# Running sums on POOL, q's squares in two fp32r parts, and low parts of 24 weight tiles by accumulating DMA, in a four-layer trunk

## The chip, the cores and the metric

One Trainium2 chip, one core in use. The metric is device time of the kernel, in microseconds, least is best. What is compared is the median of several runs of each kernel.

## The reference

Four residual layers over a sequence of 512 tokens of width 1024, in fp32. Layers 0 and 3 are Conformer convolution modules, layer 1 is attention with a forget gate, layer 2 a short gated convolution. Each is wrapped in an RMS norm and widens to 2048.

```python
def conformer_conv_mixer(h, w_in, conv_w, conv_b, ln_g, ln_b, w_out):
    proj = h @ w_in
    val, glu_gate, z = jnp.split(proj, 3, axis=-1)
    u = val * jax.nn.sigmoid(glu_gate)
    u = causal_depthwise_conv(u, conv_w) + conv_b
    u = jax.nn.silu(layer_norm(u, ln_g, ln_b))
    return (u * jax.nn.silu(z)) @ w_out
...
def forgetting_attention_mixer(h, w_in, f_bias, q_norm_g, k_norm_g, w_out):
    ...
    q = rms_norm(q.reshape(b, s_len, FOX_HEADS, FOX_HEAD_DIM), q_norm_g)
    k = rms_norm(k.reshape(b, s_len, FOX_HEADS, FOX_HEAD_DIM), k_norm_g)
    ...
for i in range(DEPTH):
    x = x + Mixer(rms_norm(x, norm))
```

The conformer's convolution has 31 taps and 2048 channels, attention has 16 heads of 128.

## The kernel before

**Tiles.** Everything is held with channels on the 128 partitions and the 512 tokens along the free axis. x is 8 tiles of 128x512, a branch 16. The weights are cut into 289 chunks of 128x1024 (512 KB): per conformer 48 for the input projection (16 each of val, gate and z) and 16 for the output, 65 + 16 for attention, 64 + 16 for the short convolution. Chunks 0 to 63 are layer 0, 225 to 288 layer 3.

**Two-part products.** A product of near fp32 accuracy is made of three fp32r products. Each chunk is loaded into w_raw (3 buffers, by SyncE's queue), ScalarE casts it to w_hi, and POOL subtracts to get w_lo = w_raw - w_hi (outside the conformers POOL or VectorE; 4 buffers each of hi and lo). The activations are split in the same way (hh and hl, or hn_hi and hn_lo after a normalisation, g_hi and g_lo ahead of the output). `project` then issues 24 matmuls for a chunk: 8 of hi by hh, 8 of hi by hl, 8 of lo by hh. With `fine` each of the 24 is planned alone, for the first tile of a layer, whose inputs come one after the other. `chunk` splits chunks AHEAD = 3 tiles before the tile that is projected.

**The plan.** Nothing runs in the order of the source. Each operation is entered with its estimated cost on the engines that can run it, a priority (its number, less a boost), its reads and writes; `Plan.trace` then simulates the engines with these costs and gives every engine its list, which it works through in order. A change of an operation, a cost or a priority can so move operations everywhere.

**Norms.** The mean of squares over channels is a sum over partitions: a matmul with a constant matrix (ones_d, ones_e in fp32, ones_hr in fp32r). `Stream.add` makes one square per x tile; in layer 0 each square goes to TensorE as a fp32 matmul of its own (ms, 8 of them), in the other layers the middle ones are first added up, leaving two.

**Conformer.** Order of tiles (`a_order`): val and gate of tile i, and from tile 9 on z of tile i - 9, so that the last nine tiles of the input projection are z alone. The first four tiles use the raw x and are multiplied by rstd afterwards, the others the normalised hn. The convolution of a tile is made of taps on VectorE (cv, into PSUM) and 7 taps on ScalarE and POOL (prod, pacc); tiles 7, 12 and 15 go to TensorE with matrices pw, through two trips to memory (ua to ud to phases, then oa to od to ob). The result of tile i is d_i. `count_in` adds d_i into s1 and its square into s2 on POOL; the last two (DIRECT = 2, tiles 14 and 15) go to TensorE directly: the layer norm's sums are meanp <- s1, d14, d15 and e2p <- s2, sq14, sq15, three fp32 matmuls each. The norm that comes out of it is applied to d, multiplied with sz = silu(z), and the output projection o starts.

**Queries.** `queries` projects a head's q, squares it and sums the squares over the 128 channels with four fp32 matmuls whose weights are the squares and whose moving operand is one column of ones (qs).

## Time and profile before

| | us |
|---|---|
| median of 3 runs | 1793.65 (1792.62 to 1793.85) |
| the profiled execution | 1794.22 |
| its span | 1792.3 |
| TensorE busy in it | 1767.3 (99%) |
| VectorE, ScalarE, POOL busy | 1167.2, 866.7, 1096.9 |
| TensorE clock granted (mean) | 0.999 |

The layers follow each other: layer 0 up to about 404 us, attention to 964, the short convolution to 1402, the second conformer to the end. Times in rows are microseconds from the start of the span. A row of the timeline gives start, length, engine, line of the code, operation, what is written and read by the program's names, shapes, a count where several are taken together, and in brackets the idle time before it and what ended that. The chain of waits is the chain of work that ended last, followed back from the last instruction. A matmul on fp32 operands is two instructions in the profile, one on fp32r operands is one.

### The profile page before, as it was taken

The numbers are of one execution on the slowest core, as the hardware profiler recorded it, in microseconds if no ns is written. First come the engines' busy times: TensorE is split into PE (matmuls) and PEld (weight loads), VectorE is DVE, ScalarE is ACT, GpSimd is POOL, SyncE is SP. The second block draws the span as 40 slices with busy tenths as digits, with TensorE's granted clock in tenths as the row PEclk, the third lists the DMA queues.
The fourth block names the chain that finished last, engine by engine and source line by source line (L and its number), as shares of the span: only waits on it lengthen the run. The fifth ranks groups of instructions, "written<-read, shape, count | busy, mean of one in ns | idle before, by whom it ended". The sixth has DMA issues, their size and how long they took to land.

```text
span 1792.3 us, 21883 instructions
## 1 busy us (share of the span) xinstructions
PE 1767.3 (99%) x8196; PEld 1462.4 (82%) x8196; DVE 1167.2 (65%) x1690; ACT 866.7 (48%) x1255; POOL 1096.9 (61%) x654
## 2 busy tenths in 40 slices
PE   8999999999999999999999999999999999999999
PEld 6788887888888888888788888888888878878787
DVE  6999997736777777867523333333313699999770
ACT  6656655536555555656433222222223564755550
POOL 5999998865333333544454555455445599989882
PEclk9999999999999999999999999999999999999999
DMA  6243432233222222222222222222223224334222
GB/s 219 83 154 99 141 135 83 94 106 118 83 78 91 85 77 85 75 77 71 71 95 94 94 94 100 101 94 95 96 100 123 88 94 147 106 129 136 94 94 71
DMA packets 63065, 182.40 MB, mean 102 GB/s; under 512 B 7136, under 2 KB 13280, under 8 KB 62960
## 3 DMA queue, kind: packets, MB, share of 16 engines
q1 hardware_dynamic: 62960, 181.02, 29.9%
q8 instruction: 64, 1.05, 0.2%
q14 instruction: 41, 0.34, 0.1%
HBM read 175.71 MB, written 5.28 MB: 101 GB/s over the span
## 4 chain that ended last, share of the span: by engine, by line
PE 81%; DVE 16%; POOL 1%; issue 1%; DMA 1%; ACT 0%; SPq 0%; DVEq 0%; POOLq 0%; ACTq 0%
PE o L379 19%; PE z L379 17%; DVE cv L341 13%; PE k L379 5%; PE v L379 5%; PE u L379 5%; PE c L379 5%; PE b L379 5%; PE q L379 5%; PE gate L379 3%; PE val L379 3%; PE cv L379 2%; PE op L379 2%; PE lg L379 2%; PE pt L874 1%
## 5 line engine op out<-in xcount | busy, mean ns | idle before, releaser
L413 POOL TENSOR_TENSOR w_lo<-w_raw,w_hi 128x1024 fp32r<-128x1024 f32 x274 | 661.1, 2414 | 586.2 <-PE z L379 110.0
L315 ACT CAST w_hi<-w_raw 128x1024 fp32r<-128x1024 f32 x289 | 303.2, 1050 | 550.9 <-issue 137.1
L341 DVE SCALAR_TENSOR_TENSOR cv<-u,vt,cv 128x495 f32<-128x495 f32 (+24 forms) x608 | 447.2, 736 | 19.7
L330 POOL TENSOR_TENSOR pacc<-prod,pacc 128x510 f32<-128x510 f32 (+5 forms) x148 | 174.7, 1181 | 11.1 <-ACT prod L317 4.4
L330 DVE TENSOR_TENSOR x<-o,x 128x512 f32<-128x512 f32 x32 | 21.2, 687 | 200.9 <-PE o L379 200.9
L317 ACT ACTIVATE prod<-u,vt 128x510 f32<-128x510 f32 (+8 forms) x166 | 106.9, 709 | 46.3 <-DVE u L330 46.3
L379 PE MATMUL o<-g_hi,w_hi 128*128 128x512 f32 x512 | 127.9, 391 | 0.7 <-DVE z L330 0.7
L379 PE MATMUL o<-g_lo,w_hi 128*128 128x512 f32 x512 | 127.0, 389 | 0.0
L379 PE MATMUL o<-g_hi,w_lo 128*128 128x512 f32 x512 | 126.7, 389 | 0.0
L379 PEld LDWEIGHTS o<-g_hi,w_hi 128*128 128x128 f32 x512 | 95.8, 188 | 21.7 <-DVE z L330 1.5
L379 PEld LDWEIGHTS o<-g_hi,w_lo 128*128 128x128 f32 x512 | 96.0, 188 | 19.9
L379 PEld LDWEIGHTS o<-g_lo,w_hi 128*128 128x128 f32 x512 | 95.9, 188 | 19.8
L246 ACT ACT_TABLE_LOAD x70 | 89.8, 1283 | 1.9 <-PEq L1030 0.7
L330 DVE TENSOR_TENSOR z<-z,rstd 128x512 f32<-128x512 f32 x32 | 22.1, 691 | 90.2 <-PE z L379 90.1
L379 PE MATMUL z<-hn_hi,w_hi 128*128 128x512 f32 x256 | 65.8, 400 | 2.2 <-ACT sz L317 2.2
L379 PE MATMUL z<-hl,w_hi 128*128 128x512 f32 x256 | 64.6, 394 | 0.0
L379 PE MATMUL z<-hn_hi,w_lo 128*128 128x512 f32 x256 | 64.3, 393 | 0.0
L379 PE MATMUL z<-hh,w_hi 128*128 128x512 f32 x256 | 64.0, 392 | 0.0
L379 PE MATMUL z<-hn_lo,w_hi 128*128 128x512 f32 x256 | 63.7, 391 | 0.0
L379 PE MATMUL z<-hh,w_lo 128*128 128x512 f32 x256 | 63.3, 389 | 0.0
L379 PEld LDWEIGHTS z<-hn_hi,w_hi 128*128 128x128 f32 x256 | 48.1, 191 | 13.9 <-ACT sz L317 3.8
L341 DVE SCALAR_TENSOR_TENSOR hl<-x,vt,hh 128x512 fp32r<-128x512 f32 x32 | 47.6, 1508 | 16.6 <-ACT hh L317 16.6
(245 smaller groups left out, 3708.1 us busy)
## 6 DMA issues: line engine op xcount, KB each, us to landing
w_raw<-w SPq DMA_DIRECT2D x289, 512.0 KB, 3.3
pw<-pw SPq DMA_DIRECT2D x54, 256.0 KB, 4.5
nc<-cd SPq DMA_DIRECT2D x16, 256.0 KB, 3.6
x<-x SPq DMA_DIRECT2D x8, 256.0 KB, 5.2
out<-x SPq DMA_DIRECT2D x8, 256.0 KB, 3.7
ud<-ua SPq DMA_DIRECT2D x6, 256.0 KB, 2.0
phases<-ud SPq DMA_DIRECT2D x24, 64.0 KB, 2.5
od<-oa SPq DMA_DIRECT2D x6, 256.0 KB, 3.9
```

Source lines behind the costliest of these rows:

```text
L246: switch(table)
L315: nc.scalar.copy(of(dst, d), of(src, s))
L317: nc.scalar.activation(of(dst, d), of(src, s), func, **kw)
L330: eng[e].tensor_tensor(of(dst, d), of(a, s), of(b, sb), op)
L341: nc.vector.scalar_tensor_tensor(of(dst, d), of(a, s), c, bb.bitcast(F32) if b_f32r else bb, op0, op1)
L379: nc.tensor.matmul(o, a, b, start=start, stop=stop)
L413: eng[e].tensor_tensor(lo(), raw(), hi().bitcast(F32), A.subtract)
L874: nc.tensor.transpose(tp()[:, blk(i - j)], p[i]()[:, blk(j)], ident())
```

## The change

Five things, with the diff below.

1. **Low parts by DMA.** From tile BY_DMA = 36 of a conformer's input projection on, chunks are split in another way: ScalarE writes -w_hi into w_lo (Copy with scale -1), and POOL issues a DMA that adds the chunk from memory into w_lo. POOL's subtraction of these chunks is gone. The plan gets an extra latency for it (`lag` 5.5) and 0.9 of POOL. As chunks are split three tiles ahead, it applies to chunks 39 to 50 and 264 to 275: the last nine z tiles and the first three of the output projection.
2. **The conformer's sums.** Only the last tile that isn't convolved on TensorE (`late`, tile 14) goes to TensorE directly; d15 and its square are added to s1 and s2 on POOL. meanp and e2p are two matmuls each.
3. **The squares of x.** In layer 0 the squares of tiles 1 to 3 are added to that of tile 0 (POOL or VectorE), which leaves 5 matmuls; in layers 1 and 2 all are added up (1 matmul); in layer 3 two remain.
4. **Order in `project`.** With `fine` the order is k = 0 to 6 of all three groups, then k = 7 of each; and the first tile on normalised inputs (n = 4) is fine too. The first loads of chunks 3 to 5 lose their priority over other loads.
5. **q's squares** are split into two fp32r parts (a cast on ScalarE, a subtraction on POOL), and qs is 8 fp32r matmuls with two columns of ones per head.

```diff
...
+BY_DMA = 36
 LAG = 9
...
-    def op(self, engines, fn, r=(), w=(), boost=0, table=None):
+    def op(self, engines, fn, r=(), w=(), boost=0, table=None, lag=0.0):
 
         o = Op()
         o.engines, o.fn, o.prio, o.table = engines, fn, len(self.ops) + boost, table
+        o.lag = lag
...
                 if len(p.engines) > 1 or e not in p.engines:
-                    late = self.LATENCY + (self.SLACK if "pe" in p.engines else 0.0)
+                    late = self.LATENCY + o.lag + (self.SLACK if "pe" in p.engines else 0.0)
                 p.ready = max(p.ready, end + late)
...
         n = state["load"]
         b = plan.buf(lambda: stage.tile([P, 1024], F32, tag="w_raw", name=f"w_raw{n}",
                                         bufs=AHEAD), "w_raw", AHEAD)
-        plan.op({"dma": 1.5}, lambda e: nc.sync.dma_start(b(), w[n]), w=[b], boost=-4000 if n >= AHEAD else 0)
+        plan.op({"dma": 1.5}, lambda e: nc.sync.dma_start(b(), w[n]), w=[b], boost=-4000 if n >= 2 * AHEAD else 0)
...
         act(hi, raw, None, cost=1.03, boost=-600)
+        parts[n] = hi, lo
+        state["split"] += 1
+        if lo_engines["now"] == ("swdge",):
+            act(lo, hi, AF.Copy, scale=-1.0, cost=1.05, boost=-600)
+            plan.op({"pool": 0.9}, lambda e: nc.gpsimd.dma_start(lo(), w[n], accum_op=A.add),
+                    [hi], [lo], boost=-600, lag=5.5)
+            return
         cost = {"dve": 1.7, "pool": 2.4}
 
         def fn(e):
             eng[e].tensor_tensor(lo(), raw(), hi().bitcast(F32), A.subtract)
         plan.op({e: cost[e] for e in lo_engines["now"]}, fn, [raw, hi], [lo], boost=-300)
-        parts[n] = hi, lo
-        state["split"] += 1
...
         hi, lo = chunk()
         hh, hl = h
-        for g, (a, b) in enumerate(((hi, hh), (hi, hl), (lo, hh))):
-            for ks in ([k] for k in range(ND)) if fine else [range(ND)]:
-                ks = list(ks)
-                mms(lambda a=a, b=b, g=g, ks=ks: [
-                        (dst(), a()[:, k * P : (k + 1) * P], b[k](),
-                         g == 0 and k == 0, g == 2 and k == ND - 1) for k in ks],
-                    [dst], pe_time(T) * len(ks), [a, *(b[k] for k in ks)], boost)
+        groups = list(enumerate(((hi, hh), (hi, hl), (lo, hh))))
+        order = [(g, range(ND)) for g in groups]
+        if fine:
+            order = [(g, [k]) for g in groups for k in range(ND - 1)]
+            order += [(g, [ND - 1]) for g in groups]
+        for (g, (a, b)), ks in order:
+            mms(lambda a=a, b=b, g=g, ks=ks: [
+                    (dst(), a()[:, k * P : (k + 1) * P], b[k](),
+                     g == 0 and k == 0, g == 2 and k == ND - 1) for k in ks],
+                [dst], pe_time(T) * len(ks), [a, *(b[k] for k in ks)], boost)
...
             self.hh[d], self.hl[d] = a, b
             sq = slot("sq")
             act(sq, xs[d], AF.Square, boost=40 if self.layer == 0 else 0)
-            if self.layer == 0 or d in (0, ND - 1):
+            if d == 0 or self.layer == 0 and d >= ND // 2 or LAYERS[self.layer] == "A" and d == ND - 1:
                 self.squares.append(sq)
             else:
                 tt(("pool", "dve"), self.squares[0], self.squares[0], sq, A.add)
...
         lo_engines["now"] = ("pool",)
         on_pe = PE_TILES[layer]
         FIRST, EARLY = 2, 7
-        raw_tiles, SPREAD, SHIFTED, DIRECT = 2, 12, 4, 2
+        raw_tiles, SPREAD, SHIFTED = 2, 12, 4
 
         def cw(i, s):
             return v(f"conv_w{layer}", i * KC + KC - 1 - s)
 
+        late = max(i for i in range(NE) if i not in on_pe)
         s1, s2, m0 = slot("s1"), slot("s2"), slot("m0")
...
             sq = slot("sq")
             act(sq, d2[i], AF.Square, boost=boost)
-            if i < NE - DIRECT:
+            if i != late:
                 tt(("pool",), s1, s1, d2[i], A.add)
                 tt(("pool",), s2, s2, sq, A.add)
             else:
...
         order = a_order()
         for n, (name, i) in enumerate(order):
             raw = n < 2 * raw_tiles
+            if n == BY_DMA:
+                lo_engines["now"] = ("swdge",)
             if n == 1:
                 st.norm(-2600, "sum")
                 normal = st.normalise(tags)
             if n == 2 * raw_tiles:
                 h = normal
             acc = psum("mm", f"{name}{layer}_{i}")
-            project(acc, h, fine=n == 0)
+            project(acc, h, fine=n == 0 or n == 2 * raw_tiles)
...
         mp, ep = psum("o", "meanp"), psum("sum", "e2p")
-        for n, (a, b) in enumerate(zip([s1] + [d2[i] for i in range(NE - DIRECT, NE)],
-                                       [s2] + last)):
+        for n, (a, b) in enumerate(zip([s1, d2[late]], [s2] + last)):
             for dst, src in ((mp, a), (ep, b)):
                 mms(lambda n=n, dst=dst, src=src: [
-                    (dst(), ones_e(), src(), n == 0, n == DIRECT)], [dst], 0.86, [ones_e, src],
+                    (dst(), ones_e(), src(), n == 0, n == 1)], [dst], 0.86, [ones_e, src],
                     boost=-2000)
...
             qh, ql = slot(f"q{h}_hi", F32R), slot(f"q{h}_lo", F32R)
             act(qh, acc, AF.Copy, scale=g, boost=-200)
             stt(ql, acc, g, qh, A.mult, A.subtract, boost=-200, b_f32r=True)
+            sp = split(sq, "sq", ("pool",))
             ms = psum("sum", f"qs{h}")
-            mms(lambda: [(ms()[:, col(j)], sq()[:, blk(j)], ones_h()[:, :1], True, True)
-                         for j in range(NB)], [ms], 0.6, [sq, ones_h])
+            mms(lambda: [(ms()[:, 2 * j : 2 * j + 2], b()[:, blk(j)], ones_hr()[:, :2],
+                          b is sp[0], b is sp[1]) for j in range(NB) for b in sp],
+                [ms], 0.5, [*sp, ones_hr])
             m, r, t = fq[h % 2]
 
             def tiny(op, *bufs, w):
                 plan.op({"dve": 0.17}, lambda _: op(), bufs, [w])
-            tiny(lambda: nc.vector.tensor_tensor(m(), ms()[:, :NB], rt2(), A.mult), ms, rt2, w=m)
+            tiny(lambda: nc.vector.tensor_tensor(m(), ms()[:, : 2 * NB : 2], rt2(), A.mult), ms, rt2, w=m)
```

How the plan moves instructions is seen on two engines. The first place is TensorE at the start of layer 0; the rows give line, operation, output<-weights' and moving operand's names (val0_0 is the first tile, hh0_k and hl0_k the parts of x, w_hi0 and w_lo0 those of chunk 0, sq a square) and the shape. Before, from the first low part of x on:

```order
L379 MATMUL val0_0_48_126<-hl0_0_22_118,w_hi0_106 128x512
L379 MATMUL ms_49_139<-sq_29_176,ones_d_10_73 128x512
L379 MATMUL ms_49_139<-sq_32_181,ones_d_10_73 128x512
L379 MATMUL val0_0_48_126<-hl0_1_25_124,w_hi0_106 128x512
L379 MATMUL ms_49_139<-sq_35_192,ones_d_10_73 128x512
L379 MATMUL val0_0_48_126<-hl0_2_28_135,w_hi0_106 128x512
L379 MATMUL val0_0_48_126<-hl0_3_31_143,w_hi0_106 128x512
L379 MATMUL val0_0_48_126<-hl0_4_34_148,w_hi0_106 128x512
L379 MATMUL ms_49_139<-sq_38_201,ones_d_10_73 128x512
L379 MATMUL ms_49_139<-sq_41_204,ones_d_10_73 128x512
L379 MATMUL ms_49_139<-sq_44_210,ones_d_10_73 128x512
```

Now, to the start of the second tile:

```order
L381 MATMUL val0_0_48_126<-hh0_6_39_153,w_lo0_112 128x512
L381 MATMUL val0_0_48_126<-hh0_7_42_165,w_hi0_106 128x512
L381 MATMUL val0_0_48_126<-hl0_7_43_172,w_hi0_106 128x512
L381 MATMUL val0_0_48_126<-hh0_7_42_165,w_lo0_112 128x512
L381 MATMUL ms_49_209<-sq_23_122,ones_d_10_73 128x512
L381 MATMUL ms_49_209<-sq_35_201,ones_d_10_73 128x512
L381 MATMUL ms_49_209<-sq_38_207,ones_d_10_73 128x512
L381 MATMUL ms_49_209<-sq_41_211,ones_d_10_73 128x512
L381 MATMUL ms_49_209<-sq_44_216,ones_d_10_73 128x512
L381 MATMUL gate0_0_78_233<-hh0_0_21_110,w_hi1_178 128x512
```

The sums ms stood between the matmuls of val0_0 as squares came; now five of them stand together behind it, k = 7 of the three groups ahead of them, and the first is that of four added squares.

The second place is TensorE at the end of layer 0's input projection (z0_12, chunk 44). Before:

```order
L379 MATMUL z0_12_351_2656<-hn0_6_lo_74_410,w_hi44_2433 128x512
L379 MATMUL z0_12_351_2656<-hn0_7_lo_77_427,w_hi44_2433 128x512
L379 MATMUL meanp_359_2560<-d14_315_2669,ones_e_11_75 128x512
L379 MATMUL e2p_360_2568<-sq_316_2679,ones_e_11_75 128x512
L379 MATMUL meanp_359_2560<-d15_324_2565,ones_e_11_75 128x512
L379 MATMUL e2p_360_2568<-sq_338_2598,ones_e_11_75 128x512
L379 MATMUL z0_12_351_2656<-hn0_0_hi_55_276,w_lo44_2522 128x512
L379 MATMUL z0_12_351_2656<-hn0_1_hi_58_296,w_lo44_2522 128x512
```

Now the running sums, 34 rows ahead of d14:

```order
L381 MATMUL z0_11_349_2618<-hn0_6_hi_73_403,w_hi43_2395 128x512
L381 MATMUL z0_11_349_2618<-hn0_7_hi_76_429,w_hi43_2395 128x512
L381 MATMUL meanp_359_2636<-s1_45_743,ones_e_11_75 128x512
L381 MATMUL e2p_360_2640<-s2_46_725,ones_e_11_75 128x512
L381 MATMUL z0_11_349_2618<-hn0_0_lo_56_319,w_hi43_2395 128x512
L381 MATMUL z0_11_349_2618<-hn0_1_lo_59_321,w_hi43_2395 128x512
```

and d14 itself:

```order
L381 MATMUL z0_12_351_2668<-hn0_6_lo_74_409,w_hi44_2441 128x512
L381 MATMUL z0_12_351_2668<-hn0_7_lo_77_436,w_hi44_2441 128x512
L381 MATMUL meanp_359_2636<-d14_315_2679,ones_e_11_75 128x512
L381 MATMUL e2p_360_2640<-sq_316_2686,ones_e_11_75 128x512
L381 MATMUL z0_12_351_2668<-hn0_0_hi_55_288,w_lo44_2527 128x512
L381 MATMUL z0_12_351_2668<-hn0_1_hi_58_305,w_lo44_2527 128x512
```

Between the second and the third group of z0_12 stood four sums, now two; s1 and s2 hold tile 15 and stand in the middle of z0_11, where they stood ahead of z0_10 before.

The third place is POOL at the same time, where the low parts of chunks 44 to 47 are made (pacc is the convolution's partial sum of tile 14, prod its products, d15 the last tile). Before:

```order
L413 TENSOR_TENSOR w_lo44_2522<-w_raw44_2325,w_hi44_2433 128x1024
L330 TENSOR_TENSOR s1_45_715<-s1_45_715,d13_296_2508 128x512
L330 TENSOR_TENSOR s2_46_717<-s2_46_717,sq_297_2524 128x512
L330 TENSOR_TENSOR pacc_304_2483<-prod_308_2198,pacc_304_2483 128x508
L413 TENSOR_TENSOR w_lo45_2570<-w_raw45_2379,w_hi45_2553 128x1024
L330 TENSOR_TENSOR d15_324_2565<-d15_324_2565,m0_47_665 128x512
L330 TENSOR_TENSOR pacc_304_2483<-prod_309_2205,pacc_304_2483 128x507
L330 TENSOR_TENSOR pacc_304_2483<-prod_310_2208,pacc_304_2483 128x506
L330 TENSOR_TENSOR pacc_304_2483<-prod_311_2220,pacc_304_2483 128x505
L413 TENSOR_TENSOR w_lo46_2628<-w_raw46_2431,w_hi46_2609 128x1024
L330 TENSOR_TENSOR pacc_304_2483<-prod_312_2225,pacc_304_2483 128x504
L330 TENSOR_TENSOR pacc_304_2483<-prod_313_2236,pacc_304_2483 128x503
```

Now:

```order
L332 TENSOR_TENSOR pacc_304_2375<-prod_313_2269,pacc_304_2375 128x503
L416 DMA w_lo44_2527<-w 128x1024
L332 TENSOR_TENSOR s1_45_743<-s1_45_743,d13_296_2546 128x512
L332 TENSOR_TENSOR d15_324_2564<-d15_324_2564,m0_47_693 128x512
L332 TENSOR_TENSOR s2_46_725<-s2_46_725,sq_297_2578 128x512
L416 DMA w_lo45_2581<-w 128x1024
L332 TENSOR_TENSOR s1_45_743<-s1_45_743,d15_324_2564 128x512
L332 TENSOR_TENSOR s2_46_725<-s2_46_725,sq_338_2586 128x512
L359 MEMSET ones_row_455_2630 128x512
L416 DMA w_lo46_2627<-w 128x1024
L416 DMA w_lo47_2677<-w 128x1024
L332 TENSOR_TENSOR d2_114_1002<-d2_114_1002,mean_361_2700 128x512
```

The subtractions became DMA issues, the sums of tiles 13 and 15 stand behind the last pacc of tile 14, and the two additions of tile 15 are new.

## The prediction

> **What bounds the kernel now.** I read the page first, then what the chain of waits is made of, then who keeps TensorE waiting once the program runs, then the busy time by stretch.

> ```profile
> PE 1767.3 (99%) x8196; PEld 1462.4 (82%) x8196; DVE 1167.2 (65%) x1690; ACT 866.7 (48%) x1255; POOL 1096.9 (61%) x654
> PE 81%; DVE 16%; POOL 1%; issue 1%; DMA 1%; ACT 0%; SPq 0%; DVEq 0%; POOLq 0%; ACTq 0%
> ```

> TensorE is busy for 99% of the span, but the chain that ended last runs through VectorE for 16% of it. That share is the convolution of the two conformers. The waits of TensorE after the first 24 us:

> ```profile
> PE cv L379 <- DMA pw<-pw: 3.7, 3, 3.1
> PE z L379 <- ACT sz L317: 2.2, 3, 1.1
> PE lg L379 <- DVE p L341: 1.9, 1, 1.9
> PE cv L379 <- DMA phases<-ud: 1.2, 2, 0.6
> ```

> The largest sum is 3.7 us of 1792, and no row names POOL's subtraction w_lo. The windows (PE, PEld, DVE, ACT, POOL busy, clock, DMA share, GB/s) show why it could still matter:

> ```profile
> 0.00:24.00 24.00, 17.20 (x47) 10.10 (x48) 10.86 (x11) 16.98 (x25) 13.12 (x21) 1.00 0.81 291
> 220.00:260.00 40.00, 39.44 (x178) 32.49 (x177) 37.89 (x53) 26.70 (x34) 37.53 (x28) 1.00 0.37 125
> 433.00:863.00 430.00, 428.07 (x2149) 361.24 (x2148) 320.33 (x598) 252.09 (x450) 173.03 (x88) 1.00 0.24 82
> ```

> In the conformer (220 to 260) VectorE and POOL are both about 94% busy, ScalarE 67%: POOL is full, yet is not waited for. In attention POOL is 40% busy. So time comes out only where TensorE's own list gets shorter and nobody else is late: a change of who makes the low parts is worth nothing by itself.

> **The change part by part.** The sum is made against the profiled execution's own 1794.22 us (span 1792.3 and 1.9 around it); the median of the three runs, 1793.65, lies 0.57 under that.

> *Fewer fp32 sums on TensorE.* Of the three kinds before:

> ```profile
> L379 PE MATMUL ms<-sq,ones_d 128*128 128x512 f32 x28 | 15.8, 665 | 0.0
> L379 PE MATMUL e2p<-sq,ones_e 128*128 128x512 f32 x8 | 4.1, 592 | 0.0
> L379 PE MATMUL meanp<-d,ones_e 128*128 128x512 f32 x8 | 4.1, 592 | 0.0
> ...
> 293.86 1.02 PE L379 MATMUL meanp<-d,ones_e 128*128 128x512 f32 x2
> 294.71 1.02 PE L379 MATMUL e2p<-sq,ones_e 128*128 128x512 f32 x2
> ```

> The counts are of instructions, two to a matmul, and from one matmul's start to the next's it is 294.71 - 293.86 = 0.85 us. The order has 9 matmuls of ms for 14 and 2 each of meanp and e2p per conformer for 3 (4 matmuls fewer over both): nine times 0.85 is 7.7 us less TensorE work. Where does it reach the end?

> *Start of layer 0 (three of the nine).*

> ```profile
> 17.51 2.74 PE L379 MATMUL ms<-sq,ones_d 128*128 128x512 f32 x6
> 20.34 0.69 ACT L317 ACTIVATE rstd<-ms,eps_t 128x512 f32<-128x512 f32 x1 [2.10 <-PE ms L379]
> 22.63 1.98 PE L379 MATMUL gate<-hh,w_hi 128*128 128x512 f32 x8
> ```

> The gate tile may begin up to 3 x 0.85 = 2.6 us earlier. But TensorE waits for x here (17.2 of 24 us busy), and the sums that go, or move behind val, were what it did meanwhile; I take -1.8, bounds -2.6 and 0. VectorE gets less: rstd starts when the last sum ends, and that is now just ahead of gate, so about 20.1 to 21 instead of 20.3.

> *Conformer tails (two each).* The end of the first, where VectorE's last convolution meets TensorE:

> ```profile
> 290.79 0.75 DVE L341 SCALAR_TENSOR_TENSOR d<-cv,vt,pacc 128x512 f32<-128x512 f32 x1 [0.49 <-POOL pacc L330]
> 291.58 0.63 ACT L317 ACTIVATE sq<-d 128x512 f32<-128x512 f32 x1 [0.56 <-DVE d L341]
> 315.45 1.98 PE L379 MATMUL o<-g_hi,w_hi 128*128 128x512 f32 x8
> ...
> 297.45 18.16 PE z L379 x80
> ```

> The square of d14 is there at 292.2, TensorE comes for d14 at 293.86: 1.6 us of slack. (The last row is the chain's: 80 matmuls in 18.16 us, 0.227 each, 5.44 to a weight tile of 24.) The order leaves the same work between the convolution of tile 15 and d14, so the two sums that fall out behind d14 are gained whole, -1.7. What TensorE gained before (start) passes only up to that 1.6 us, since VectorE is bound and its own start doesn't come forward. Start and tail together: **-3.0** (-1.7 - 1.3; bounds -4.3 and -0.7).

> In layer 3 there is no start to gain, and d14 stands one group of eight earlier (8 matmuls, 1.8 us):

> ```profile
> 1676.88 0.63 ACT L317 ACTIVATE sq<-d 128x512 f32<-128x512 f32 x1
> 1679.80 1.02 PE L379 MATMUL meanp<-d,ones_e 128*128 128x512 f32 x2
> ```

> Of the 2.3 us of slack 0.5 is left. I take **-1.5** (bounds -2.3 and -0.5).

> *What the tails newly wait for.* d15 now goes through POOL's running sums, and TensorE takes s1, s2 about 9 us ahead of d14.

> ```profile
> 270.53 0.59 ACT L315 COPY oa<-cv 128x512 f32<-128x512 f32 x1 [9.01 <-PE cv L379]
> 275.20 0.38 SPq L399 DMA_DIRECT2D w_raw<-w  x1
> 279.84 1.23 ACT L648 ACTIVATE d<-ob,vt 128x512 f32<-128x512 f32 x1 [1.47 <-DMA ob<-od]
> ...
> 1656.49 0.59 ACT L315 COPY oa<-cv 128x512 f32<-128x512 f32 x1 [7.04 <-PE cv L379]
> 1662.86 1.21 ACT L648 ACTIVATE d<-ob,vt 128x512 f32<-128x512 f32 x1
> L330 POOL TENSOR_TENSOR s<-s,d 128x512 f32<-128x512 f32 x26 | 33.6, 1293 | 10.6 <-DVE d L341 10.2
> ```

> From oa to the end of d15 it is 10.5 us in layer 0, with a load of w_raw (second row) between the four transfers of ob, which the new order has behind them, and 7.6 in layer 3. Behind d15 come four POOL operations of 1.29 in layer 0 and three in layer 3, and one DMA issue: 12.8 to 15.7 us and 11.5, plus the issue. TensorE comes for s2 64 matmuls and one sum after tile 15 in layer 0 (15.4 us), 56 and one in layer 3 (13.6). I take no wait, bounds 0 and +2.7 per conformer (an issue of 2.4).

> *Transitions.* ms falls from two matmuls to one ahead of layers 1 and 2: **-1.7**. With k = 7 last in each first tile TensorE should have cover for the last x; no row of waits names these tiles, so 0 (0 to -0.4 each).

> *Queries.* fp32 128x1 matmuls become 8 fp32r of two columns per head, as many instructions as before:

> ```profile
> 442.66 0.19 PEld L379 LDWEIGHTS lg<-k_lo,q_hi 128*128 128x128 f32 x1
> 442.77 0.19 PEld L379 LDWEIGHTS lg<-k_hi,q_lo 128*128 128x128 f32 x1
> 442.88 0.97 PEld L379 LDWEIGHTS qs<-ones_h,sq 128*128 128x128 f32 x8
> ```

> fp32r loads behind small operands follow each other at 0.11 us, and so do the fp32 ones of qs (0.97 less 0.19, over 7). I take **0**, bounds -6 (0.4 a head) and +2.5 from more waits such as lg's 1.9. The added cast (0.6) and POOL subtraction (1.4) lengthen the way to qs; its users stand about 20 us behind it.

> [...]

> *Low parts by DMA.* By the order it is chunks 39 to 50 and 264 to 275: nine z tiles and the first three output tiles of each conformer, since chunks are split three tiles ahead.

> ```profile
> L413 POOL TENSOR_TENSOR w_lo<-w_raw,w_hi 128x1024 fp32r<-128x1024 f32 x274 | 661.1, 2414 | 586.2 <-PE z L379 110.0 <-ACT w_hi L315 81.1 <-PE o L379 73.7
> L315 ACT CAST w_hi<-w_raw 128x1024 fp32r<-128x1024 f32 x289 | 303.2, 1050 | 550.9 <-issue 137.1 <-PE z L379 125.4 <-PE o L379 119.6
> w_raw<-w SPq DMA_DIRECT2D x289, 512.0 KB, 3.3
> ```

> ScalarE gains 24 x 1.05 = 25 us, POOL loses 24 x 2.41 = 58 and pays 24 issues (each between SP's 0.4 and the 2.4 that it replaces). Both lie beside TensorE. The transfer: a plain load of the size lands in 3.3 us; the accumulating one also reads its target, so I bound it by 3.3 and 9.9 (three such streams) and take 6.6. With four buffers, from the end of one low group to the start of the fourth after it there are 4 x 5.44 - 1.81 = 19.9 us. ScalarE's copy (1.05 and up to 2 of wait) and POOL's queue (up to two operations of 2.4) leave at least 12.1. So **0**. It can help: a raw buffer is free after the cast, so the loads of pw behind it on SP start earlier (part of the 3.7 us of waits); I take -0.5.

> [...]

> **Sum.** -3.0 - 1.7 - 1.5 + 0 + 0 - 0.5 = -6.7: 1794.2 becomes 1787.5; against the median 1787.0, which I give.

> **The rivals.** *The transfers are late (slower).* Place: the low groups of the z tiles from 39 on. For it: POOL works in order, and no row shows such a transfer. Against it: the 12 us left. It decides from 12 to 15 us of landing. At 16.5 (five plain loads) with 1.5 and 3.6 us of queues it is 22.7 us for 19.9, 0.7 a tile, over 24 tiles +16: about 1803. *VectorE holds both conformers* (95% busy there, 16% of the chain): of the tails and the start nearly nothing passes, or s2 is waited for; transitions and half of one tail remain, -2.6: 1791. [...] *Not what it says*: the title's last 12 in-projection tiles are nine and three; at a cover as long in the output tiles this alters no term.

> **How the numbers follow.** Forecast 0.55, VectorE holds 0.20, transfers late 0.14, cheaper qs 0.11. A measurement tells 0.2% (3.6 us) from no change: below 1790.1 lie the forecast but for 0.03, cheaper qs, and 0.04 of VectorE's case, 0.67; within, 0.19; above, 0.14. The range from 1780.5 takes in the cheaper qs and to 1796 the waits of both tails; it leaves out the late transfers and half of the cheaper qs.

> **What would show it.** The gate of layer 0 at about 21 us; meanp's d14 in layer 0 near 292.5 and o at 312.5; ms x2 at each transition; qs still 0.9 us a head; no wait of z or o for the DMA of w_lo, and its landing under 12 us. Wrong if TensorE waits for s2 or for w_lo, or if another stall of the two conformers takes the 3 us.

## The result, and the profile after

The change makes the kernel slower: 1809.78 us (median of 5 runs, 1808.22 to 1814.01) against 1793.65 (5 runs, 1792.19 to 1795.82), a ratio of 1.0096 [1.0079, 1.0113]. The profiled execution took 1808.22 us, 14.0 more than that of before, and its span 1806.5. The page's busy times, its chain by engine, and the new transfer with its median time to landing:

```profile
PE 1765.8 (98%) x8178; PEld 1459.5 (81%) x8178; DVE 1156.2 (64%) x1686; ACT 896.7 (50%) x1295; POOL 1106.2 (61%) x683
PE 70%; DVE 23%; DMA 2%; issue 2%; ACT 2%; POOL 1%; SPq 0%; DVEq 0%; ACTq 0%; POOLq 0%
w_lo<-w POOLq DMA_DIRECT2D x24, 512.0 KB, 5.5
```

TensorE has 18 instructions fewer (8178 for 8196), the nine fp32 sums of the forecast, worth 7.7 us. But the chain now runs through VectorE for 23% where it was 16%, and POOL, for which 24 subtractions became issues of a DMA, is busier than before (1106.2 for 1096.9). The waits of TensorE after the first 24 us (in total, times, longest) say where to look:

```profile
PE pt L888 <- DVE p L352: 8.5, 11, 0.9
PE cv L381 <- DMA pw<-pw: 4.6, 4, 3.8
PE z L381 <- ACT sz L319: 4.2, 3, 2.3
PE meanp L381 <- POOL s L332: 3.1, 2, 1.9
PE cv L381 <- DVE cv L343: 2.5, 2, 1.7
```

The first row is new, and it lies in attention. The low parts by DMA are named in no row. Cut at the first matmul of each stage (starts from the trace), the spans differ so:

| stage | before | after | difference |
|---|---|---|---|
| layer 0, input projection | 308.88 | 312.52 | +3.64 |
| layer 0, output projection | 87.04 | 87.04 | 0 |
| attention, with its output projection | 559.11 | 568.78 | +9.67 |
| short convolution (input, output) | 349.92, 88.59 | 349.04, 88.55 | -0.92 |
| layer 3, input projection | 301.29 | 302.84 | +1.55 |
| layer 3, output projection | 86.81 | 86.81 | 0 |

The sum is 13.94 of the 14.0. One thing has to be known to read such spans. The windows of the profile give the clock that was granted to TensorE: it is 1.00 but for stretches of 3.41 us, or twice that, at 0.50, and each 3.41 us so spent takes up to 1.7 us from TensorE. Ahead of its last microseconds the execution of after has three such stretches, at 289.12 (layer 0's input projection), 763.57 (attention) and 1661.28 (layer 3's input projection); that of before has one, at 1596.90 (layer 3's input projection). Each comes behind a wait of TensorE (in after of 1.87, 1.84 and 3.82 us, in before of 3.12); the last section says when.

There are two questions: what happened in attention, where no TensorE work was added, and why both conformers got longer with less to sum.

**Attention.** What pt waits for is VectorE's rescaling of the softmax rows p by 1/rsum, a line that the change does not touch. The four widths by form (busy time, mean ns of one, idle before), first before, then after:

```profile
L350 DVE TENSOR_SCALAR p<-p,rsum 128x512 f32<-128x512 f32 x16 | 8.8, 552 | 0.6
L350 DVE TENSOR_SCALAR p<-p,rsum 128x256 f32<-128x256 f32 x16 | 7.6, 476 | 0.6
L350 DVE TENSOR_SCALAR p<-p,rsum 128x384 f32<-128x384 f32 x16 | 7.6, 473 | 0.6
L350 DVE TENSOR_SCALAR p<-p,rsum 128x128 f32<-128x128 f32 x16 | 4.6, 287 | 0.6
```

```profile
L352 DVE TENSOR_SCALAR p<-p,rsum 128x128 f32<-128x128 f32 x16 | 19.0, 1187 | 0.6
L352 DVE TENSOR_SCALAR p<-p,rsum 128x256 f32<-128x256 f32 x16 | 16.0, 1003 | 0.6
L352 DVE TENSOR_SCALAR p<-p,rsum 128x512 f32<-128x512 f32 x16 | 10.7, 668 | 0.6
L352 DVE TENSOR_SCALAR p<-p,rsum 128x384 f32<-128x384 f32 x16 | 9.6, 599 | 0.6
```

The same 64 instructions took 28.6 us and now take 55.3, and the smallest grew most, from 287 ns to 1187. What came on top, 0.90 us at 128x128 and 0.12 at 128x512, does not go by the size of the instruction, so I took it for waiting inside it. The timeline of after shows for what (start, length, engine):

```profile
566.45 2.40 POOL L422 TENSOR_TENSOR w_lo<-w_raw,w_hi 128x1024 fp32r<-128x1024 f32 x1 [2.51 <-ACT p L319]
...
567.22 1.78 DVE L352 TENSOR_SCALAR p<-p,rsum 128x256 f32<-128x256 f32 x1
...
568.81 1.32 POOL L368 TENSOR_TENSOR sq_lo<-sq,sq_hi 128x512 fp32r<-128x512 f32 x1
...
569.10 1.10 DVE L352 TENSOR_SCALAR p<-p,rsum 128x128 f32<-128x128 f32 x1
...
570.26 0.98 PE L888 MATMUL pt<-ident,p 128*128 128x128 f32 x7 [0.90 <-DVE p L352]
```

POOL's w_lo ends at 568.85 and the rescaling beside it at 569.00; POOL's sq_lo, the subtraction of k's squares, ends at 570.13 and the next rescaling at 570.20, upon which TensorE's pt follows after 0.90 us of idling. I went through all 64 in this way, with 0.286, 0.353, 0.420 and 0.486 us as the undisturbed lengths of the four widths (the last rescaling above takes 1.10 us for 0.286). In after 25 start while one of POOL's TENSOR_TENSOR operations runs, and all 25 end behind it, by their own length less 0.20 us. Thirteen are held by w_lo, eleven by sq_lo (seven of k, four of q), one by ncm. The other 39 start while POOL makes none, and no one of them is longer than 489 ns. In before 4 start beside such an operation; 3 are held, and the fourth, which meets only the last 0.16 us of it, is not. The excess sums to 30.6 us against 3.9. The stretch at half speed at 763.57 is not what attention lost: the changed kernel without the DMA (below) has no such stretch in attention, and takes 568.71 us there.

**Conformers.** VectorE is what binds layer 0's convolution. Its windows from 46 to 290 us are alike, first before, then after (TensorE, weight loads, VectorE, ScalarE, POOL busy):

```profile
46.00:290.00 244.00, 239.64 (x1152) 199.06 (x1151) 232.84 (x323) 146.77 (x197) 228.40 (x164) 1.00 0.36 120
```

```profile
46.00:290.00 244.00, 236.24 (x1137) 196.27 (x1136) 233.10 (x324) 153.72 (x205) 220.48 (x167) 1.00 0.43 133
```

VectorE is at 95% in both. So what counts is when its chain of convolutions begins. In before that was here:

```profile
38.30 2.33 DVE L341 SCALAR_TENSOR_TENSOR cv<-u,vt,cv 128x511 f32<-128x511 f32 x3
```

In after it is later, and the rows ahead of it say why:

```profile
15.15 5.58 POOL L422 TENSOR_TENSOR w_lo<-w_raw,w_hi 128x1024 fp32r<-128x1024 f32 x2
15.66 2.87 DVE L332 TENSOR_TENSOR sq<-sq,sq 128x512 f32<-128x512 f32 x1
18.58 4.56 PE L381 MATMUL ms<-sq,ones_d 128*128 128x512 f32 x10 [1.68 <-DVE sq L332]
22.57 2.39 PE L381 MATMUL gate<-hh,w_hi 128*128 128x512 f32 x8
23.17 0.69 ACT L319 ACTIVATE rstd<-ms,eps_t 128x512 f32<-128x512 f32 x1 [0.53 <-PE ms L381]
43.15 0.74 DVE L343 SCALAR_TENSOR_TENSOR cv<-u,vt,cv 128x511 f32<-128x511 f32 x1
```

An addition of two squares takes 2.87 us beside POOL's two subtractions (the same form on VectorE, k times rstd at 566.42, takes 0.69); TensorE's five sums wait 1.68 us for it, rstd starts at 23.17 instead of 20.34, and the first convolution at 43.15 instead of 38.30. The gate tile, which was to come 1.8 us sooner, starts at 22.57 for 22.63. The end of this chain:

```profile
263.24 5.59 PE L381 MATMUL cv<-phases,pw 128*128 128x128 f32 x48 [1.68 <-DVE cv L343]
272.20 0.59 ACT L317 COPY oa<-cv 128x512 f32<-128x512 f32 x1 [9.56 <-PE cv L381]
275.39 0.88 POOL L416 DMA_DIRECT2D w_lo<-w  x1 [2.39 <-ACT w_lo L319]
282.50 1.22 ACT L659 ACTIVATE d<-ob,vt 128x512 f32<-128x512 f32 x1 [3.84 <-DMA ob<-od]
288.50 1.50 PE L381 MATMUL meanp<-s,ones_e 128*128 128x512 f32 x2 [1.87 <-POOL s L332]
292.97 0.75 DVE L343 SCALAR_TENSOR_TENSOR d<-cv,vt,pacc 128x512 f32<-128x512 f32 x1
```

TensorE waits 1.68 us for VectorE ahead of tile 15, so oa is at 272.20 (270.53 before), d15 is back from memory at 282.50 (279.84), and the sums that now need d15 keep TensorE waiting for 1.87 us. d14 is at 292.97, 2.2 later than before. Of the 3.64 us that layer 0's input projection got longer, some 1.7 are the stretch at half speed that follows the wait for s.

### The profile page after: what moved, and what is told of

The parts are those of the page before. It is cut to its first block, busy times and chain, and to the rows that moved or that the text cites. A ratio compares the mean times of both kernels' runs of the same rounds, so it can differ in the third digit from the quotient of the medians.

```text
span 1806.5 us, 21962 instructions
## 1 busy us (share of the span) xinstructions
PE 1765.8 (98%) x8178; PEld 1459.5 (81%) x8178; DVE 1156.2 (64%) x1686; ACT 896.7 (50%) x1295; POOL 1106.2 (61%) x683
## 3 DMA queue, kind: packets, MB, share of 16 engines
q8 instruction: 64, 1.05, 0.2%
## 4 chain that ended last, share of the span: by engine, by line
PE 70%; DVE 23%; DMA 2%; issue 2%; ACT 2%; POOL 1%; SPq 0%; DVEq 0%; ACTq 0%; POOLq 0%
PE o L381 19%; DVE cv L343 17%; PE z L381 14%; PE c L381 5%; PE u L381 5%; PE b L381 5%; PE k L381 5%; PE q L381 4%; PE v L381 4%; DVE p L352 2%; PE gate L381 2%; PE op L381 2%; PE lg L381 1%; PE val L381 1%; PE cv L381 1%
## 5 line engine op out<-in xcount | busy, mean ns | idle before, releaser
L422 POOL TENSOR_TENSOR w_lo<-w_raw,w_hi 128x1024 fp32r<-128x1024 f32 x257 | 620.9, 2417 | 525.9 <-PE o L381 81.0
L317 ACT CAST w_hi<-w_raw 128x1024 fp32r<-128x1024 f32 x289 | 303.1, 1049 | 560.8 <-issue 126.6
L332 POOL TENSOR_TENSOR pacc<-prod,pacc 128x510 f32<-128x510 f32 (+5 forms) x148 | 177.2, 1198 | 11.5 <-ACT prod L319 4.5
L381 PE MATMUL cv<-phases,pw 128*128 128x125 f32 (+8 forms) x432 | 53.5, 282 | 9.2 <-DMA pw<-pw 4.6
L381 PEld LDWEIGHTS cv<-phases,pw 128*128 128x128 f32 x432 | 51.9, 197 | 12.7 <-issue 6.3
## 6 DMA issues: line engine op xcount, KB each, us to landing
w_raw<-w SPq DMA_DIRECT2D x289, 512.0 KB, 3.2
w_lo<-w POOLq DMA_DIRECT2D x24, 512.0 KB, 5.5
```

The costliest lines, as they stand in the source:

```text
L317: nc.scalar.copy(of(dst, d), of(src, s))
L332: eng[e].tensor_tensor(of(dst, d), of(a, s), of(b, sb), op)
L381: nc.tensor.matmul(o, a, b, start=start, stop=stop)
L422: eng[e].tensor_tensor(lo(), raw(), hi().bitcast(F32), A.subtract)
```

## The experiments

Each is timed in 5 rounds beside the kernel before; the ratio is to that. Stage spans and rows are of its profiled execution. "From after" takes something out of the changed kernel, "from before" puts one part of the change alone into the kernel before.

### Attention: q's squares

**From after, q's squares as before.**

```diff
-            sp = split(sq, "sq", ("pool",))
...
-                          b is sp[0], b is sp[1]) for j in range(NB) for b in sp],
-                [ms], 0.5, [*sp, ones_hr])
+            mms(lambda: [(ms()[:, col(j)], sq()[:, blk(j)], ones_h()[:, :1], True, True)
+                         for j in range(NB)], [ms], 0.6, [sq, ones_h])
```

> The changed kernel with q's squares as before (four fp32 matmuls of one column, no cast, no subtraction on POOL). Theory 1 (POOL's subtractions hold up VectorE's rescaling of p in attention): the 64 rescalings fall from 55.3 us to about 30, TensorE's waits of pt for p from 8.5 us to under 1, the kernel gains 8 to 11 us, about 1800. Rival (the waits come from the rest of the plan's new order, not from the subtraction of q's squares): the waits stay above 5 us and the time is within 3 us of 1809.8.

1802.45 us, 1.0052 [1.0039, 1.0065]: 7.3 less than after. No wait of pt is left, the 64 rescalings are back at 28.6 us, and attention takes 558.2 (q 457.47 for after's 471.41), 10.6 less than after. The whole gains less, since layer 0's input projection takes 317.31 us in this execution, with 3.4 us lost to half speed where after loses 1.7.

**From before, q's squares alone** (the reverse of that diff).

> The kernel of before with q's squares in two fp32r parts (low part on POOL), nothing else. Theory 1: attention alone gets longer, by 8 to 11 us, with 7 to 10 us of pt's waits for p and the rescalings held by POOL as in the changed kernel; 1802 to 1805. Rival (the loss needs the other edits, which move the plan): within 3 us of before.

1803.29 us, 1.0045 [1.0028, 1.0061]. Layer 0 stays (308.59, first convolution at 38.51); attention takes 569.5, 10.4 more than before. The same wait stands at the head of its list:

```profile
PE pt L876 <- DVE p L350: 8.5, 11, 1.0
```

So this part alone makes the whole loss in attention. It could still be the added subtraction itself, or what the plan does around it.

**From after, q's subtraction on VectorE.**

```diff
-            sp = split(sq, "sq", ("pool",))
+            sp = split(sq, "sq", ("dve",))
```

> The changed kernel with the low part of q's squares made on VectorE in place of POOL, all else the same, 8 fp32r matmuls for qs too. Theory 1: no rescaling of p is held by a subtraction of q's squares; the rescalings take 30 to 42 us in place of 55.3, pt's waits fall below 3 us, 5 to 10 us gained, 1800 to 1805. Rival (the longer way to qs, or qs's new place on TensorE, makes pt late, whatever engine subtracts): waits and time as with POOL, 1807 to 1812.

1815.69 us, 1.0126 [1.0110, 1.0141], no better and rather worse, which I had not expected:

```profile
PE pt L888 <- DVE p L352: 11.0, 15, 0.9
```

The excess of the rescalings is 35.3 us: they are held by w_lo 16 times, by k's sq_lo 7 times and by ncm twice. So it isn't q's subtraction as such. POOL's low parts of weights between 433 and 863 us, first before, then in this kernel, show what else moved:

```profile
L413 POOL TENSOR_TENSOR w_lo<-w_raw,w_hi 128x1024 fp32r<-128x1024 f32 x49 | 118.1, 2411 | 218.3 <-PE z L379 64.4 <-ACT qr L824 55.4 <-PE q L379 47.4
```

```profile
L422 POOL TENSOR_TENSOR w_lo<-w_raw,w_hi 128x1024 fp32r<-128x1024 f32 x58 | 139.6, 2407 | 192.6 <-ACT r L319 43.5 <-ACT p L319 43.4 <-PE q L381 34.0
```

With more to do for q the plan gives POOL 9 of VectorE's low parts, and w_lo holds 16 rescalings, 2 before (in after it is 57 low parts, and 13).

**From after, the rescaling on ScalarE.** That leaves POOL's order of work to the plan and takes the disputed operation off VectorE.

```diff
-                ts(p[i], p[i], (rsum[i], slice(0, 1)), A.mult, s=s)
+                act(p[i], p[i], AF.Copy, s=s, scale=(rsum[i], slice(0, 1)))
```

> The changed kernel with p's rescaling (times 1/row sum) on ScalarE (Copy with a scale) in place of VectorE's TENSOR_SCALAR; q's low parts stay on POOL. Theory 1 (VectorE's rescaling can't start while a POOL subtraction runs): ScalarE has no such wait, TensorE's waits of pt for p fall from 8.5 us to under 2, attention (first q to first u) falls from 562.9 us to about 552 to 555, the kernel to 1798 to 1803. Rival (the longer way to qs or the plan's order makes p itself late): pt goes on waiting for p, over 5 us, the kernel stays above 1806.

1803.46 us, 1.0049 [1.0032, 1.0066]; attention 560.3 for after's 568.8 and before's 559.1, and no wait of pt is left. (Half speed takes 3.4 us of attention here, none in before.) The 64 rescalings on ScalarE, beside the same kind of POOL work:

```profile
L319 ACT ACTIVATE p<-p,rsum 128x512 f32<-128x512 f32 (+1 forms) x64 | 32.9, 553 | 1.4 <-DVE rsum L880 1.2
```

With q's new sums in place and only the engine of p changed, the loss goes. This, with the ends of the 25, shows that it is VectorE's rescaling held by POOL.

### The low parts by DMA

**From after, no DMA** (POOL subtracts as before).

```diff
-BY_DMA = 36
+BY_DMA = 1000
```

> The changed kernel with all low parts of the conformers subtracted on POOL, no accumulating DMA. Theory 2 (the DMA's issue waits in POOL's queue for ScalarE's copy, and its transfer delays ob and with it d15): meanp's wait for POOL's s1 and s2 falls from 3.1 us to under 1 in both conformers together, d15 comes about 6 to 7.5 us behind od in place of 8.5 and 9.7, 3 to 7 us gained, about 1805. Rival (the running sums with tile 15 are late by themselves): the wait stays at 2 to 5 us, and the time is within 2 us of 1809.8. Attention should keep its pt waits (7 to 10 us) either way.

1813.76 us, 1.0111 [1.0095, 1.0126], where I had expected about 1805: not told from after (1.0096 [1.0079, 1.0113]). The wait of meanp for s is gone, but the work is back on POOL, which is full here (94% in before's window of 46 to 290 us), and d14 and the output projection wait for it:

```profile
298.62 0.75 DVE L343 SCALAR_TENSOR_TENSOR d<-cv,vt,pacc 128x512 f32<-128x512 f32 x1 [5.69 <-POOL pacc L332]
```

```profile
318.06 3.78 PE L381 MATMUL o<-g_hi,w_hi 128*128 128x512 f32 x8 [4.97 <-ACT g_hi L317]
```

So taking the DMA out exchanges one wait for another; whether it helps within the whole change, these intervals do not tell. Alone it costs:

**From before, the DMA alone** (the part of the diff in `chunk`, with BY_DMA and lag).

> The kernel of before with the low parts of chunks 39 to 50 and 264 to 275 by accumulating DMA, nothing else. Theory D (POOL stands at each DMA issue until ScalarE's copy is done, which waits for a free low buffer, and the sums behind it in POOL's queue are late; ob comes back later beside the transfers): TensorE waits 2 to 5 us for POOL's s or for d15, the two conformers' projections take 612 to 620 us for before's 610.2, the kernel 1796 to 1803. Rival (POOL is only relieved): 606 to 610 us, 1790 to 1794.

1801.62 us, 1.0045 [1.0033, 1.0057]; input projections 312.28 (308.88) and 303.24 (301.29). Again nothing waits for the DMA of w_lo, nor do the sums wait for POOL's s, which I had expected. What waits is z for ScalarE:

```profile
233.71 1.95 ACT L319 ACTIVATE prod<-u,vt 128x511 f32<-128x511 f32 x3 [3.93 <-DVE u L332]
...
237.59 1.05 ACT L319 ACTIVATE w_lo<-w_hi 128x1024 fp32r<-128x1024 f32 x1
...
242.53 1.04 ACT L319 ACTIVATE w_lo<-w_hi 128x1024 fp32r<-128x1024 f32 x1
...
247.05 0.60 ACT L319 ACTIVATE sz<-z 128x512 f32<-128x512 f32 x1
...
247.70 3.60 PE L381 MATMUL z<-hn_hi,w_hi 128*128 128x512 f32 x8 [2.41 <-ACT sz L319]
```

In before ScalarE takes up the same prod at 233.47, 0.24 us sooner, and from there works through to sz without a pause of half a microsecond, at 244.96. Now two copies of 1.05 us stand between, and sz is at 247.05, 2.1 later. TensorE's z tile, for which sz has to read out a tile before it, waits 2.41 us for 0.56. The other 1.7 of the 3.4 us that layer 0's projection got longer are the clock: it stands at 0.50 from 247.94 for 3.41 us.

**From that, POOL adds instead of the DMA.** ScalarE's copy of -w_hi stays, the transfer goes.

```diff
-            plan.op({"pool": 0.9}, lambda e: nc.gpsimd.dma_start(lo(), w[n], accum_op=A.add),
-                    [hi], [lo], boost=-600, lag=5.5)
+            plan.op({"pool": 2.4}, lambda e: nc.gpsimd.tensor_tensor(
+                lo(), raw(), lo().bitcast(F32), A.add), [raw, hi], [lo], boost=-600)
```

> The kernel of before with the same chunks split by ScalarE's negated copy and a POOL addition of w_raw in place of the DMA: the copy's cost without the transfer. If ScalarE's copy makes sz late (theory C), z waits for ScalarE's sz 2 to 4 us as with the DMA (3.5 in layer 0), the two conformers' projections take 613 to 617 us and the kernel 1797 to 1802. If the transfer or the DMA's issue does it, 608 to 611 us and 1792 to 1795, with no new wait.

1800.36 us, 1.0035 [1.0023, 1.0048]; input projections 313.10 and 303.06, as with the DMA. The wait has moved by one operation of ScalarE's list:

```profile
PE z L381 <- ACT sg L319: 5.1, 2, 3.2
```

The loss stays without any transfer: most of it comes with the copy on ScalarE, or with the new order around it. (POOL's addition here also has a higher priority than the subtraction of before, a boost of -600 for -300; that was not tried by itself.)

### The start of layer 0

**From after, the start as before** (each square of layer 0 to TensorE alone, all k of a group in turn, chunks 3 to 5 loaded first again).

```diff
-            if d == 0 or self.layer == 0 and d >= ND // 2 or LAYERS[self.layer] == "A" and d == ND - 1:
+            if d == 0 or self.layer == 0 or LAYERS[self.layer] == "A" and d == ND - 1:
...
-            project(acc, h, fine=n == 0 or n == 2 * raw_tiles)
+            project(acc, h, fine=n == 0)
```

> The changed kernel with the start as before: eight squares of layer 0 to TensorE, k in order in the first tile, chunk loads 3 to 5 with priority, the first normalised tile in groups. Theory 3 (the start gains nothing, since TensorE waits for x and the sums filled its waits): gate of layer 0 begins within 1 us of before's 22.6, and the time is within 3 us of 1809.8. Rival (the start's new order delays VectorE's first convolution and with it the whole first conformer): VectorE's first cv comes 1 to 3 us earlier, 2 to 4 us gained, about 1806.

1813.35 us, 1.0110 [1.0096, 1.0124]. The first convolution comes at 39.27 instead of 43.15 and d14 at 291.2 instead of 293.0, as it should; yet pw waits of 3.6 and meanp waits of 3.4 us take their place, and the input projection is 315.91. Undoing a loss does not return it here: the plan lays the rest out anew, and two stretches at half speed fall into this projection where after has one.

**From before, the start alone** (parts 3 and 4 of the change).

> The kernel of before with the new start alone: squares of x added up, k = 7 last in fine tiles, priority of the first loads. Theory V (the sum of squares now comes behind an addition on VectorE that POOL holds up; rstd is late, and VectorE, which sets the first conformer's length, starts its convolution late): VectorE's first cv at 42 to 48 us for 38.3, d14 and the output projection of layer 0 later by 3 to 8, 1.8 us less at the two transitions, the kernel 1795 to 1800. Rival (the start's 2.6 us of sums are gained): cv at 36 to 38, 1788 to 1791.

1803.47 us, 1.0050 [1.0038, 1.0062]. The first convolution is at 45.58, rstd at 25.60, d14 at 301.08; layer 0's input projection takes 313.98, with a wait of 3.73 us for g_hi at its end. The output projection behind it takes 90.02 for 87.04, and that is the clock: from 320.26 on it stands at 0.50 for 6.83 us, which takes 3.0 us. Attention takes 2.3 more than before, though its transition gains 0.9: two stretches at half speed lie in it.

**From before, layer 0's added squares alone, and the order of k and loads alone.**

```diff
-            if self.layer == 0 or d in (0, ND - 1):
+            if d == 0 or self.layer == 0 and d >= ND // 2 or self.layer and d == ND - 1:
```

> The kernel of before with the squares of x tiles 1 to 3 in layer 0 added to tile 0's, nothing else. Theory V (the addition on VectorE and POOL makes the sum late): rstd's first step on ScalarE later than 20.3 us by 2 to 5, first cv at 41 to 46, 1796 to 1802. Rival (the order and the loads do it): cv at 37 to 39, 1791 to 1794.

1799.06 us, 1.0027 [1.0016, 1.0039]: rstd at 25.85 for 20.34, first convolution at 45.83, layer 0 312.38. POOL makes the additions here, and the sums start behind them, at 20.74 for 8.21.

```diff
-        plan.op({"dma": 1.5}, lambda e: nc.sync.dma_start(b(), w[n]), w=[b], boost=-4000 if n >= AHEAD else 0)
+        plan.op({"dma": 1.5}, lambda e: nc.sync.dma_start(b(), w[n]), w=[b], boost=-4000 if n >= 2 * AHEAD else 0)
...
+            order = [(g, [k]) for g in groups for k in range(ND - 1)]
+            order += [(g, [ND - 1]) for g in groups]
...
-            project(acc, h, fine=n == 0)
+            project(acc, h, fine=n == 0 or n == 2 * raw_tiles)
```

> The kernel of before with k = 7 last in fine tiles, the first normalised tile fine, and the loads of chunks 3 to 5 without priority; all squares as before. Theory V: first cv at 37 to 40 us, 1791 to 1795. Rival: cv at 41 to 46 us, 1796 to 1802.

1801.71 us, 1.0038 [1.0026, 1.0051]: time and first convolution (41.83) fall where the rival had put them, not where I had. It is not the squares' way, for rstd is at 20.52 as before; and the first tile's d is only 0.9 late (84.15 for 83.23). But d14 is late by 7.7, because POOL's sums for it are:

```profile
298.51 0.75 DVE L341 SCALAR_TENSOR_TENSOR d<-cv,vt,pacc 128x512 f32<-128x512 f32 x1 [7.63 <-POOL pacc L330]
```

Both halves lose, one by VectorE's late start, the other by POOL's list in the last tiles. Why the plan orders pacc so much worse there I did not follow further.

### The running sums and the transitions

**From after, the sums as before** (DIRECT = 2, three matmuls each).

```diff
-            if i != late:
+            if i < NE - DIRECT:
```

> The changed kernel with the conformer's sums as before: tiles 14 and 15 to TensorE directly, meanp and e2p three matmuls each again. Theory 2b (in both conformers the sums of tile 15 on POOL are late, since d15 comes back from memory late): no wait of meanp for POOL's s (3.1 us with the change), 3.4 us more matmuls, the two conformers' projections together 1 to 4 us shorter than with the change (615.4 us), the kernel 1806 to 1809. Rival (the conformers lose by VectorE's later start and the waits for pw, whoever sums): the two together 616 to 620 us, the kernel 1810 to 1814. Attention as with the change.

1813.70 us, 1.0104 [1.0083, 1.0125], not told from after, as the rival had it. The sums still wait for POOL, 3.2 us for e2p; the first convolution of this execution is at 47.39.

**From before, the sums alone; the transitions alone; both.** The first and third put part 2 of the change into before, the second only this:

```diff
-            if self.layer == 0 or d in (0, ND - 1):
+            if d == 0 or self.layer == 0 or LAYERS[self.layer] == "A" and d == ND - 1:
```

> The kernel of before with d15 and its square in the running sums on POOL (two matmuls each of meanp and e2p), nothing else. Theory S (POOL is full in the conformers, so two more additions make the last pacc and with it d14 late, as without the DMA in the changed kernel): VectorE waits 2 to 6 us for POOL's pacc at d14, the output projection of layer 0 starts late or waits for g_hi, the kernel 1796 to 1802. Rival (3.4 us of matmuls go and nothing is late): 1790 to 1792.

> The kernel of before with all squares of x added up on POOL or VectorE ahead of layers 1 and 2 (one fp32 matmul of ms in place of two), nothing else. The transitions' term: 0.9 us less at each, 1791.9 against 1793.7; the conformers and attention as before. Rival (the one sum comes later and delays rstd, so attention's start waits): nothing gained, 1793 to 1795.

> The kernel of before with the one-matmul sums of squares ahead of layers 1 and 2 and the running sums with tile 15. If their gains add: 1.8 us at the transitions and 0 to 2 in the conformers, 1790 to 1792. If the later d14 (2 us of VectorE waiting for POOL at the end) takes it back: 1792 to 1794.

The sums: 1793.79, 0.9996 [0.9988, 1.0005]. Input projections 306.41 and 298.29, 2.5 and 3.0 shorter (1.7 of the 3.0 are before's stretch at half speed in layer 3, which this execution has not); but their output projections take 88.73 and 88.53, 1.7 each more, with small waits for VectorE's g_lo at their start. Attention takes 3.2 more, and that is the clock alone: TensorE idles 3.86 us in it as before, but two stretches at half speed, at 758.99 and 871.63, take 3.4. The transitions: 1793.88, 0.9993 [0.9982, 1.0004]. Both: 1793.47, 0.9995 [0.9986, 1.0003]. No version here can be told from before on the good side.

**From before, the DMA and the sums.**

> The kernel of before with both, DMA and running sums, and neither start nor q. If the two only help each other (the DMA frees POOL for the additions): 610 to 614 us in the two conformers, 1793 to 1797. If the waits of POOL's queue remain: 614 to 620 us, 1797 to 1804, with 2 to 4 us of meanp's waits for s.

1804.99 us, 1.0060 [1.0048, 1.0072], not clearly more than the DMA alone (1.0045 [1.0033, 1.0057]). z waits for sz as above, and now meanp for s:

```profile
288.91 1.12 PE L381 MATMUL meanp<-s,ones_e 128*128 128x512 f32 x2 [1.71 <-POOL s L332]
```

Here VectorE's start is that of before. So the wait for s does not need a late start: the DMA and the running sums are enough. Alone on before, the parts cost 9 (q), 7.5 (DMA), 9.4 (start) and nothing (sums, transitions), 26 in all where the whole costs 16. They do not add: start, DMA and sums meet in the same conformers, where VectorE and POOL are full (95% and 94% in before's window of 46 to 290 us). Nor is each of these costs that of its own stage alone, as the stretches at half speed in attention show for DMA (1.6 us in its profiled execution) and start (3.2).

## Why the prediction was wrong

*What bounds the kernel.* That an engine which is full only in the conformer is free elsewhere was the first mistake. "In attention POOL is 40% busy" was right and is no measure of what POOL does to VectorE: a busy share counts what POOL takes, not what it keeps another engine from, here 30.6 us of longer rescalings on VectorE.

*Queries, 0, bounds -6 and +2.5: the step that failed most, +10.5* (attention's 9.67 and the 0.88 of its transition). The 0 itself was right for TensorE: qs stays eight instructions a head, at the pitch of before, 0.11 us:

```profile
566.18 0.25 PE L381 MATMUL qs<-ones_hr,sq_hi 128*128 128x2 f32 x1
...
566.29 0.25 PE L381 MATMUL qs<-ones_hr,sq_lo 128*128 128x2 f32 x1
```

So qs did not get cheaper. No run shows the 0.4 us a head behind the bound of -6, the chance of 0.11 and the low end of the range; a weight load of qs takes 187 to 192 ns in fp32r (after) and 188 to 192 in fp32 (before). What failed was the bound of +2.5, taken from one old wait (lg's 1.9). The step asked who stands behind the added cast and subtraction in data ("its users stand about 20 us behind it"), and not which operation of VectorE would run at the same time as POOL's. The three held rescalings of before were in the trace, each 0.8 to 2.0 us too long.

*Start and tail, -3.0: became +3.6 over layer 0's input projection.* The forecast priced what TensorE loses (sums) and said that VectorE "gets less": rstd at 20.1 to 21. It is 23.17, since the square that TensorE now waits for is added on VectorE beside POOL's w_lo. The stage is VectorE's, so this passes on toward its end (d14 2.2 us late), while three sums less on TensorE brought the gate forward by 0.06 us. The two sums less in the tail were gained, and the waits ate them. And a wait cost more than its length: behind that for s TensorE ran at half speed for 3.41 us, 1.7 us for which the forecast had no term.

*Layer 3, -1.5: became +1.55* (both executions have one stretch at half speed there), with a wait for s (1.20), one for sz (2.3 in all, of 0.6 before) and a longer one for pw (3.8, of 3.1).

*Waits for s2, forecast none, bounds to +2.7 each: 1.87 and 1.20 us.* Inside the bounds, on the wrong side of the choice. The way of d15 from oa to its end was taken over from before as 10.5 us in layer 0; it is 11.5, and it starts 1.7 later. In layer 3 it went from 7.6 to 10.3.

*Transitions, -1.7: right* by the stages: layers 1 and 2 start 0.88 us sooner each (the gates of attention 5.91 for 6.79, the short convolution 349.04 for 349.92). Alone, in the time of the whole, it could not be told.

*Low parts by DMA, transfer 0: right. Earlier loads, -0.5: not seen* (pw waits 4.6 us, 3.7 before). Landing in 5.5 us (5.0 to 8.2 by the transfer's own row) lies between the bounds of 3.3 and 9.9, and nothing waits for it. The rival that the transfers are late falls. But "Both lie beside TensorE" was wrong for ScalarE's 25 us: it is 67% busy there, and what counts is not its share but that sz stands behind two copies in its list. The DMA alone costs 7.5 us and the copy without the transfer 6, half-speed stretches included.

*The rivals.* That VectorE holds both conformers was the nearest in kind, but priced as a lost gain (-2.6), with no way to lose. The loss in attention was in none.

## What to carry to other kernels

An engine with idle time is not free to take work if its operations hold up another engine's, as POOL's held 25 of VectorE's rescalings here, by up to 2.17 us each: before moving work to POOL, list VectorE's operations of the same stretch, and look in the trace for ones whose length does not go by their size. A copy added to an engine that works in order costs what stands behind it (sz came 2.1 us later behind two copies), so name that operation and who waits for it, however low the busy share. A wait of TensorE can cost more than its length (up to 1.7 us more behind the one of 1.87): look at the granted clock behind it, and look at it too before a difference of 1.7 or 3.4 us between stages is laid to the edit. And in a stage that another engine binds, ask of each saving on TensorE what it does to the start of the binding engine's chain; there a planner that does not know that POOL holds up VectorE, or lays everything out anew, can lose more than the saved work is worth.

## What the runs showed of the hardware that I had not expected

Behind some of its waits TensorE came back at half speed. The eight matmuls at 247.70 with the DMA alone, behind a wait of 2.41 us, take 3.60 us for 2.12 before, the eight at 318.06 without the DMA, behind 4.97 us, 3.78. The windows show it (TensorE, weight loads, VectorE, ScalarE, POOL busy, clock, DMA share, GB/s), first in after, around its wait of 1.87 us for s:

```profile
285.71:289.12 3.41, 1.54 (x7) 0.72 (x5) 3.23 (x6) 3.02 (x5) 3.41 (x4) 1.00 0.40 53
289.12:292.53 3.41, 3.41 (x7) 1.58 (x6) 3.27 (x5) 0.00 (x0) 1.85 (x3) 0.50 1.01 267
```

then with the order of k and the loads alone, around a wait of 3.73 us for g_hi, behind which the first eight matmuls take 2.14 and the clock stays at 1.00:

```profile
312.67:316.08 3.41, 1.50 (x7) 0.92 (x5) 3.38 (x5) 2.82 (x4) 3.41 (x3) 1.00 0.48 154
316.08:319.49 3.41, 1.59 (x7) 1.31 (x8) 3.33 (x5) 1.94 (x3) 0.81 (x2) 1.00 0.42 154
```

POOL's additions right behind its own DMA issue are longer here: of after's 56 additions into s1 and s2, 11 take 1.47 to 1.59 us, all in a run of additions directly behind an issue, and the other 45 take 1.27 to 1.32 (before's 52 take 1.26 to 1.31). The two of d15 into s1 and s2 take 1.56 and 1.55 us where the one ahead of them, of a square into s2, takes 1.31:

```profile
285.05 1.31 POOL L332 TENSOR_TENSOR s<-s,sq 128x512 f32<-128x512 f32 x1
286.89 1.56 POOL L332 TENSOR_TENSOR s<-s,d 128x512 f32<-128x512 f32 x1
288.12 1.55 POOL L332 TENSOR_TENSOR s<-s,sq 128x512 f32<-128x512 f32 x1
```

The two start 1.23 us apart, as the first and the issue do, so each ends a quarter of a microsecond later for it: that much lies on the way to the wait for s. Whether the issue or the transfer behind it does this was not tried.
